# Holding four engines of the merge of a diffusion layer to the written order

## Chip, core and metric

The kernel runs on one core of one Trainium2 chip. The metric is device time in microseconds (us) from a launch of the whole layer, as the median of several runs. The profile is of one execution.

## What is computed

One layer over 2048 latent tokens of width 1024, with a context of 256 tokens. The part that the change touches is `branch_merge` and the residual behind it, and in the kernel the first operations of the channel sub-layer:

```python
def branch_merge(attn_o, gm_o, ga_logit, gb_logit, w_br_attn, w_br_gm, w_out):
    y = jax.nn.sigmoid(ga_logit) * (attn_o @ w_br_attn) + jax.nn.sigmoid(gb_logit) * (gm_o @ w_br_gm)
    return y @ w_out
...
    x = x + g1 * branch_merge(attn_x, gm_x, ga_x, gb_x, w_br_attn[l], w_br_gm[l], w_out[l])
    h2 = modulate(x, norm2_g[l], sh2, sc2)
    x = x + g2 * sq_relu_mlp(h2, w_ff1[l], w_ff2[l])
```

Here `attn_o` and `gm_o` are 2048 x 512, `w_br_attn` and `w_br_gm` 512 x 1024, `w_out` 1024 x 1024. Ahead of it lie the input projection, attention and the gated spatial mixing; behind it the MLP of width 4096.

## The kernel before

All matmuls take fp32 data as two rounded parts, a high part h and a remainder l = x - h, and make each product of three matmuls (`mm3`: h h, h l, l h). So each operand has a cast to h (ScalarE, L144, in some places VectorE) and a subtraction for l (L148, on GpSimd or VectorE): the function `split`.

The tokens are taken in four blocks (b = 0 to 3) of 512. In `merge` each block has two stages.

The first is the *branch product*. For each of eight steps m (128 output columns) TensorE makes two products in PSUM, of gated mixing ("g") and then of attention ("a"), each over four chunks k of the contraction: 24 matmuls of 128x512. VectorE multiplies both by their gates (L910, twice) and adds them (L913). ScalarE casts the sum to the high part of y, and GpSimd makes its remainder. Ahead of the matmuls of step m, `fetch` loads the raw weights and gates of two steps later and splits the weights: for each of "g" and "a" a cast on ScalarE and a remainder on GpSimd (on VectorE where block 0 calls it). Steps are counted through here, 0 to 31: block 1 has 8 to 15. Weights, raw and split, have the tag `bw` with 14 buffers (a step takes two raw and four split ones), gates have `gt` with 6.

The second is the *output product*, y times `w_out`. For each of four token tiles tt and two halves n of the columns, TensorE makes 24 matmuls over the eight parts of y. Of the first tile the parts 0 to 6 are taken for both halves ahead of part 7. After each half VectorE multiplies by the adaLN gate (L954) and adds to the residual tile `xt` (L955), and then `next(side, None)` issues one step of a side job. After each tile the sum goes to memory and ScalarE takes its sum of squares (L960).

In blocks 0 to 2 the side job is `br_inputs` of the next block: eight steps, one for each chunk of the branch inputs. Each loads a raw tile (and, for attention, a row of reciprocals, by which VectorE multiplies it in L848), casts it on ScalarE and makes the remainder on VectorE. The tag is `raw` (3 buffers) for what is loaded and `in` (16) for the parts.

In block 3 the side job is `h_early`, the head of the channel sub-layer for the first half of the tokens. Four of its steps begin with `turn(kk)`: VectorE scales a tile of 128 x 2048 (L992 in `h_scaled`), TensorE makes 16 transposes of it (L182), ScalarE takes the four results out of PSUM (L999). The other pieces (`combine`, `done`, `h_last`, `w1_plain`, `w1_combine`) are sums and splits on VectorE and ScalarE. The turns come after the first half of tile 0, the first half of tile 1, and both halves of tile 2:

```python
                    nc.vector.tensor_tensor(out=part, in0=ps, in1=self.g1b[:, cs], op=ALU.mult)
                    nc.vector.tensor_tensor(out=xt[:, cs], in0=xt[:, cs], in1=part, op=ALU.add)
                    next(side, None)
```

The program is a list of instructions in the written order. A planner then sets the order on each engine and on each DMA queue from modelled costs, with the written order as priority. `order` binds some of it by dependencies that cost no semaphore: buffers of one tag are first written in the written order, and an instruction that is "held" goes behind the one written before it on its engine. In the kernel before, held are a few short ranges (`pins`), TensorE and VectorE in attention (`fixed`), and SyncE in the second product of the MLP (`loads`). Nothing is held in `merge`. Transfers in `merge` are issued by SyncE, apart from the softmax sums, which ScalarE issues within block 0's branch product.

Of the kernel before, what the change touches and what calls it, by code (L numbers as in the profile page):

```python
# [67 lines left out]
class Kern:  # L68
    def __init__(self, ctx, tc, I, out):
        self.tc, self.nc, self.I, self.out = tc, tc.nc, I, out  # L70
        self.ctx = ctx
        self.uid = 0
        self.tags = {}
        self.pins = []
        self.fixed = []
        self.loads = []
        self.open_pools, self.pool_of = {}, {}
        self.banks = None
# [799 lines left out]
    def merge(self, first, start, last):  # L878
        nc = self.nc
        for _ in start:  # L880
            pass
        self.close("mid", "base")
        self.open("out")
        self.open("branch")
        steps = [(b, m) for b in range(NB) for m in range(KC)]
        it = iter(steps)
        q = []
        w_out = self.load_w_out()

        def fetch(lo_eng="pool"):  # L890
            s = next(it, None)
            if s is not None:
                q.append((self.br_weights(self.br_raw(s[1]), lo_eng), self.gate_in(*s)))

        inp = first
        early = [(s, self.br_raw(s[1])) for s in (next(it), next(it))]
        for s, raw in early:
            q.append((self.br_weights(raw, "dve"), self.gate_in(*s)))
        for b in range(NB):
            y = []  # L900
            for m in range(KC):
                fetch("pool" if b else "dve")
                ws, gt = q.pop(0)
                for nm in ("g", "a"):
                    ps = self.bank([TB])
                    wh, wl = ws[nm]
                    for k in range(4):
                        h, l = inp[nm][k]
                        self.mm3(ps, wh[:, k, :], wl[:, k, :], h, l, k == 0, k == 3)
                    nc.vector.scalar_tensor_tensor(  # L910
                        out=gt[nm], in0=gt[nm], scalar=1.0, in1=ps, op0=ALU.add, op1=ALU.mult
                    )
                nc.vector.tensor_tensor(out=gt["a"], in0=gt["a"], in1=gt["g"], op=ALU.add)  # L913
                yh, yl = self.sb("y", [TB], F32R), self.sb("y", [TB], F32R)
                self.split(gt["a"], yh, yl)
                y.append((yh, yl))
                if b == 0:
                    next(w_out, None)
                    if m == 2:
                        last.sums(self.sb("raw", [TB]))  # L920
                    if m == 4:
                        last.inverse()
            inp = {}
            if b + 1 < NB:
                side = self.br_inputs(b + 1, inp)
            else:
                self.close("branch", "pre")
                self.open("early", side="right")
                side = self.h_early()
                next(side)  # L930
            for tt in range(TT):
                tok = slice(tt * P, (tt + 1) * P)
                xt = self.sb("xt", [D])
                nc.sync.dma_start(xt, self.x_block(b)[tok, :])
                banks = [self.bank([512]) for _ in range(2)]

                def outer(n, ks):
                    cs = slice(n * 512, (n + 1) * 512)
                    for k in ks:
                        self.mm3(  # L940
                            banks[n], y[k][0][:, tok], y[k][1][:, tok], self.wo[k][0][:, cs],
                            self.wo[k][1][:, cs], k == 0, k == KC - 1,
                        )

                head = KC - 1 if tt == 0 else KC
                if tt == 0:
                    for n in range(2):
                        outer(n, range(head))
                for n in range(2):
                    cs = slice(n * 512, (n + 1) * 512)  # L950
                    ps = banks[n]
                    outer(n, range(head if tt == 0 else 0, KC))
                    part = self.sb("jk", [512])
# [3 lines that stand above are left out]
                nc.sync.dma_start(self.x1_d[b][tok, :], xt)  # L957
                junk = self.sb("jk", [D], mybir.dt.bfloat16)
                col = b * TT + tt
                nc.scalar.activation(  # L960
                    junk, xt, AF.Square, accum_out=self.ss2[:, col : col + 1]
                )
            for _ in side:
                pass

    def halves(self, kk, p, raw):
        nc = self.nc
        tag = "he" if (kk, p) in EARLY else "hl"
        h, l = self.sb(tag, [TB], F32R), self.sb(tag, [TB], F32R)
        nc.scalar.copy(h, raw)  # L970
        nc.vector.tensor_tensor(out=l, in0=raw, in1=f32(h), op=ALU.subtract)  # L971
        return h, l
# [469 lines left out]
    def order(self):  # L1442
        dep = mybir.DependencyInfo(mybir.DependencyClass.NoSync, mybir.DependencyReason.DATA)
        last, seen = {}, set()
        pinned = {n for r in self.pins for n in r}
        fixed = {n for r in self.fixed for n in r}
        loads = {n for r in self.loads for n in r}
        engines = (self.nc.tensor.engine, self.nc.vector.engine)
        for idx, i in enumerate(list(self.nc.cur_bb.bb.instructions)):
            keys = []  # L1450
            for o in i.outs:
                n = getattr(getattr(o, "bass_ap", None), "name", None)
                if n in self.tags and n not in seen:
                    seen.add(n)
                    keys.append(self.tags[n])
            held = idx in pinned or (idx in fixed and i.engine in engines)
            held = held or (idx in loads and i.engine == self.nc.sync.engine)
            after = keys + ([i.engine] if held else [])
            for prev in {last[k].name for k in after if k in last}:
                self.tc.add_manual_dep(i, prev, dep, reason="order")  # L1460
            for k in keys + [i.engine]:
                last[k] = i
# [242 lines left out]
```

## Time and profile before

| what | value |
|---|---|
| median of 3 runs | 3123.49 us (3121.77 to 3127.06) |
| the profiled execution | 3121.05 us |
| its span, first to last instruction | 3119.3 us |
| mean granted TensorE clock | 0.995 |
| TensorE busy | 3045.5 us (98%) |
| VectorE busy | 1937.7 us (62%) |
| ScalarE busy | 1352.0 us (43%) |
| GpSimd busy | 917.5 us (29%) |

The granted clock is the share of the full TensorE clock. PE is TensorE's matmul, PEld its weight load, DVE is VectorE, ACT ScalarE, POOL GpSimd, SP SyncE (SPq its queue of transfers). A line number such as L954 is that of the listing. In the profile `bw<-bw,bw` stands for the buffers that an instruction writes and reads, without their numbers. Matmul records overlap, so that TensorE's rate is better read from the distance of starts than from one duration. A bracket in a row of the timeline gives the engine's idle time ahead of the instruction and what ended it.

### The profile page before, as it was taken

What the parts mean: (1) busy time and instruction counts of PE and PEld (TensorE: products, weight loads), DVE (VectorE), ACT (ScalarE), POOL (GpSimd) and SP (SyncE); (2) the same over time, 40 slices, a digit from 0 to 9 for tenths busy, and PEclk for the clock granted to TensorE, in tenths of its full rate; (3) what the DMA queues carried; (4) which work ended last, traced back from release to release, by engine and by line L of the source; (5) the groups of instructions that cost most, each with busy time, mean ns of one, the idle gap of its engine ahead of it and who ended that gap; (6) DMA issues with size and microseconds to landing.
All of it is one profiled execution on the core that took longest, in us unless ns stands there. A gap on an engine that the chain in (4) does not pass through costs nothing.

```text
span 3119.3 us, 38046 instructions
## 1 busy us (share of the span) xinstructions
PE 3045.5 (98%) x13892; PEld 2299.1 (74%) x13892; DVE 1937.7 (62%) x2797; ACT 1352.0 (43%) x2058; POOL 917.5 (29%) x635
## 2 busy tenths in 40 slices
PE   7999999999999999999999999999999999999999
PEld 4888788877655555555777877887777788888777
DVE  4735666576677777677643478876654576654445
ACT  3353434433545454545322244444543344444433
POOL 1423324241688888888133300000000000000000
PEclk9999999999999999999999999999999999999999
DMA  6353555535100000002855448888576644445565
GB/s 202 112 177 119 200 166 172 188 93 188 38 14 5 18 11 18 11 5 91 272 161 161 151 145 314 313 306 280 190 259 204 216 149 154 158 147 194 206 215 203
DMA packets 332174, 485.42 MB, mean 156 GB/s; under 512 B 33969, under 2 KB 166321, under 8 KB 331986
## 3 DMA queue, kind: packets, MB, share of 16 engines
q1 hardware_dynamic: 324002, 478.38, 46.0%
q10 hardware_dynamic: 7984, 4.61, 0.5%
q8 instruction: 109, 1.79, 0.2%
q14 instruction: 79, 0.65, 0.1%
HBM read 348.56 MB, written 134.35 MB: 155 GB/s over the span
## 4 chain that ended last, share of the span: by engine, by line
PE 79%; DVE 7%; DMA 6%; POOL 3%; ACT 2%; issue 2%; SPq 0%; ACTq 0%; DVEq 0%; POOLq 0%
PE b L1196 12%; PE b L1197 12%; PE b L1195 11%; PE b L1597 8%; PE b L176 7%; PE b L178 7%; PE b L177 7%; PE b L1564 5%; PE b L1583 4%; PE b L1529 3%; PE b L182 2%; DMA bw<-in_w_br_gm 1%; DMA w<-in_w_in 1%; DVE f L1292 1%; DMA f<-ao_d 1%
## 5 line engine op out<-in xcount | busy, mean ns | idle before, releaser
L1292 DVE TENSOR_TENSOR f<-f,f 128x1024 fp32r<-128x1024 f32 x224 | 272.9, 1223 | 269.3 <-ACT f L1291 265.3
L1540 DVE TENSOR_REDUCE ts<-b 128x1 f32<-128x512 f32 x512 | 314.5, 681 | 172.6 <-PE b L1529 172.6
L1291 ACT CAST f<-f 128x1024 fp32r<-128x1024 f32 x224 | 235.2, 1053 | 330.8 <-DMA f<-ao_d 293.2
L1196 PE MATMUL b<-f,f 128*128 128x512 f32 x896 | 350.8, 392 | 5.1 <-DVE f L1292 4.6
L1197 PE MATMUL b<-f,f 128*128 128x512 f32 x896 | 348.9, 389 | 0.0
L1613 POOL TENSOR_TENSOR ac<-ac,p 128x512 f32<-128x512 f32 x216 | 296.3, 1403 | 70.7 <-ACT p L1587 69.5
L1195 PE MATMUL b<-f,f 128*128 128x512 f32 x896 | 306.6, 391 | 10.2 <-ACT b L1334 4.5
L1587 ACT ACTIVATE p<-b 128x512 f32<-128x512 f32 x384 | 199.6, 616 | 156.2 <-PE b L1583 153.4
L148 POOL TENSOR_TENSOR w<-w,w 128x1024 fp32r<-128x1024 f32 x60 | 148.6, 2477 | 399.5 <-ACT w L144 169.3
L1613 POOL TENSOR_TENSOR ac<-ac,t 128x512 f32<-128x512 f32 x160 | 232.5, 1478 | 0.1
L1196 PE MATMUL b<-hl,f 128*128 128x512 f32 x576 | 225.3, 391 | 2.2 <-DVE hl L971 2.1
L1195 PE MATMUL b<-hl,f 128*128 128x512 f32 x576 | 224.6, 390 | 0.0
L1197 PE MATMUL b<-hl,f 128*128 128x512 f32 x576 | 224.3, 390 | 0.0
L144 ACT CAST w<-w 128x1024 fp32r<-128x1024 f32 x120 | 125.9, 1049 | 217.4 <-DMA w<-in_w_in 181.3
L176 PE MATMUL b<-t,w 128*128 128x512 f32 x512 | 204.2, 399 | 5.7 <-DVE t L590 5.4
L1195 PEld LDWEIGHTS b<-f,f 128*128 128x128 f32 x896 | 167.5, 188 | 50.8 <-ACT f L1291 7.0
L1196 PEld LDWEIGHTS b<-f,f 128*128 128x128 f32 x896 | 168.2, 188 | 46.5 <-DVE f L1292 12.2
L178 PE MATMUL b<-t,w 128*128 128x512 f32 x512 | 200.9, 392 | 0.0
L177 PE MATMUL b<-t,w 128*128 128x512 f32 x512 | 200.5, 392 | 0.0
L1564 PE MATMUL b<-t,t 128*128 128x512 f32 x576 | 197.8, 413 | 0.8 <-ACT p L1587 0.5
L178 PE MATMUL b<-w,t 128*128 128x512 f32 (+1 forms) x528 | 192.0, 364 | 2.6 <-POOL t L148 2.5
L1197 PEld LDWEIGHTS b<-f,f 128*128 128x128 f32 x896 | 168.2, 188 | 34.4
(228 smaller groups left out, 6461.6 us busy)
## 6 DMA issues: line engine op xcount, KB each, us to landing
w<-in_w_in SPq DMA_DIRECT2D x120, 512.0 KB
ao_d<-f SPq DMA_DIRECT2D x224, 256.0 KB
f<-ao_d SPq DMA_DIRECT2D x112, 512.0 KB
f<-w2o_d SPq DMA_DIRECT2D x112, 512.0 KB
f<-in_w_ff SPq DMA_DIRECT2D x48, 1024.0 KB
w2o_d<-f SPq DMA_DIRECT2D x112, 256.0 KB
md<-in_w_mod SPq DMA_DIRECT2D x32, 512.0 KB
f<-x_d SPq DMA_DIRECT2D x64, 256.0 KB
```

What stands on the lines that cost most here:

```text
L176: mm(ps, sh, mh, start=start, stop=False)
L177: mm(ps, sh, ml, start=False, stop=False)
L178: mm(ps, sl, mh, start=False, stop=stop)
L1195: mm(ps, wh, hh, start=start and k == 0, stop=False, skip_group_check=True)
L1196: mm(ps, wh, hl, start=False, stop=False, skip_group_check=True)
L1197: mm(ps, wl, hh, start=False, stop=k == len(w) - 1, skip_group_check=True)
L1291: nc.scalar.copy(h, f32(l))
L1292: nc.vector.tensor_tensor(out=l, in0=f32(l), in1=f32(h), op=ALU.subtract)
L1540: nc.vector.tensor_reduce(out=self.mx[:, t, h, c : c + 1], in_=ps[h], axis=AX.X, op=ALU.max)
L1564: self.nc.tensor.matmul(self.pts[j][h], k.KA[c][self.kv][:, ks], self.qa[h], start=True, stop=False, skip_group_check=True,)
L1597: nc.tensor.matmul(self.o[h * HD : (h + 1) * HD, :], k.V[c][:, i, self.kv * HD : (self.kv + 1) * HD], pt[h], start=j == 0, stop=j == NKT - 1,)
L1613: nc.gpsimd.tensor_tensor(out=self.acc[e][:, h], in0=old[:, h], in1=pt[h], op=ALU.add)
```

## The change

A list `steady` gets one range: from the end of block 0's branch product to the end of `merge`. In `order` each instruction in that range is held behind the one written before it on its engine, except those on SyncE. No instruction is added, removed or changed.

```diff
@@ def __init__
         self.fixed = []
+        self.steady = []
         self.loads = []
@@ def merge
                     if m == 4:
                         last.inverse()
+            if b == 0:
+                begin = self.here()
             inp = {}
...
             for _ in side:
                 pass
+        self.steady.append(range(begin, self.here()))
@@ def order
         loads = {n for r in self.loads for n in r}
+        steady = {n for r in self.steady for n in r}
...
             held = idx in pinned or (idx in fixed and i.engine in engines)
+            held = held or (idx in steady and i.engine != self.nc.sync.engine)
             held = held or (idx in loads and i.engine == self.nc.sync.engine)
```

## The prediction

> **What bounds the kernel now.** I read the page first, for the engine that fills the span, then the busy time by stretch over the merge, then the waits of TensorE in it, and last the timelines around those waits.
>
> ```profile
> PE 3045.5 (98%) x13892; PEld 2299.1 (74%) x13892; DVE 1937.7 (62%) x2797; ACT 1352.0 (43%) x2058; POOL 917.5 (29%) x635
> ```
>
> TensorE is busy 98% of the span, so an edit counts only by the TensorE idle time, or slow TensorE time, that it takes away or adds. The stretches below are, in order, the output product of block 0, then branch products and output products of blocks 1 to 3, then the start of the channel sub-layer. Columns: stretch, its length, busy time of PE, PEld, DVE, ACT and POOL, granted clock, DMA share, GB/s.
>
> ```profile
> 1521.53:1565.05 43.52, 43.52 (x193) 36.05 (x192) 22.99 (x32) 11.66 (x21) 4.47 (x3) 1.00 0.70 234
> 1565.05:1608.57 43.52, 43.52 (x193) 36.05 (x192) 16.80 (x23) 11.33 (x20) 21.48 (x17) 1.00 0.49 151
> 1608.57:1659.87 51.30, 46.31 (x193) 36.88 (x192) 22.44 (x29) 11.64 (x20) 9.58 (x8) 0.97 0.56 180
> 1703.39:1755.03 51.64, 47.39 (x194) 37.61 (x193) 20.94 (x29) 11.62 (x20) 9.64 (x8) 0.93 0.49 163
> 1755.03:1798.55 43.52, 43.52 (x194) 36.05 (x193) 18.25 (x24) 10.90 (x19) 22.68 (x17) 1.00 0.52 161
> 1798.55:1849.13 50.58, 50.58 (x257) 42.85 (x256) 40.43 (x62) 21.28 (x34) 1.32 (x1) 1.00 0.37 122
> 1849.13:1880.70 31.57, 26.63 (x98) 18.27 (x97) 27.97 (x41) 19.27 (x32) 0.00 (x0) 0.95 0.61 211
> ```
>
> Each stretch of 192 matmuls takes 43.52 us undisturbed (0.227 us each; eight steps of 5.44 us). TensorE already runs the stages one behind the other in the written order. Two stretches are long: the output products of blocks 1 and 2 lose 51.30 - 43.52 = 7.78 and 51.64 - 43.52 = 8.12 us, together 15.9. Block 3's output product loses nothing: 50.58 is 192 matmuls plus 64 transposes.
>
> ```profile
> PE b L176 <- ACT y L144: 6.5, 2, 3.5
> PE b L178 <- POOL y L148: 2.6, 4, 1.0
> ```
>
> These two rows are all that TensorE waits for from 1522 to 1849 us: the casts and remainders of y, the last two of a block. The ScalarE timeline says why they are late:
>
> ```profile
> 1535.56 1.14 ACT L144 CAST bw<-bw 128x512 fp32r<-128x512 f32 x2
> 1607.68 0.62 ACT L144 CAST y<-gt 128x512 fp32r<-128x512 f32 x1
> 1612.04 0.62 ACT L144 CAST bw<-bw 128x512 fp32r<-128x512 f32 x1 [3.75 <-DMA bw<-in_w_br_gm]
> 1614.09 0.62 ACT L144 CAST bw<-bw 128x512 fp32r<-128x512 f32 x1 [1.43 <-POOL bw L148]
> 1614.61 1.13 ACT L144 CAST in<-raw 128x512 fp32r<-128x512 f32 x2
> 1615.65 0.61 ACT L144 CAST y<-gt 128x512 fp32r<-128x512 f32 x1
> 1618.92 0.62 ACT L144 CAST bw<-bw 128x512 fp32r<-128x512 f32 x1 [2.14 <-DMA bw<-in_w_br_gm]
> 1620.98 0.62 ACT L144 CAST bw<-bw 128x512 fp32r<-128x512 f32 x1 [1.44 <-POOL bw L148]
> 1624.16 0.62 ACT L144 CAST y<-gt 128x512 fp32r<-128x512 f32 x1 [2.04 <-DVE gt L913]
> ```
>
> The y casts of steps 14 and 15 (15 is the last of block 1) stand behind weight casts (bw) that wait for transfers, and behind input casts of the next block. The weight pairs run one step ahead of the text: from 1535.56 to 1618.92 there are nine pairs, steps 10 to 18, and the text has only steps 10 to 17 before y of step 15.
>
> **The change part by part.** No instruction is added or removed. On four engines, from block 0's output product to the end of the merge, each instruction goes behind the one written before it; SyncE's queue stays the planner's. So the parts are moves.
>
> *(a) The scaling at the head of each turn of `h_early`.* The lines, vector rows first:
>
> ```profile
> 1804.10 2.29 DVE L992 TENSOR_TENSOR f<-f,fs 128x2048 f32<-128x2048 f32 x1
> 1808.95 0.69 DVE L954 TENSOR_TENSOR jk<-b,g 128x512 f32<-128x512 f32 x1 [2.56 <-PE b L178]
> 1809.56 2.28 DVE L992 TENSOR_TENSOR f<-f,fs 128x2048 f32<-128x2048 f32 x1
> ...
> 1808.52 0.39 PE L178 MATMUL b<-wo,y 128*128 128x512 f32 x1
> 1808.75 1.91 PE L182 MATMUL b<-ident,f 128*128 128x128 f32 x16
> ```
>
> The text has, after the matmuls of a half n: L954, L955, L992, then 16 transposes, then the next half's matmuls. The planner keeps TensorE in that order but puts L992 (1804.10) ahead of L954 (1808.95), so the transposes start without a wait. Held in the written order, L954 must wait for the half's last matmul, L992 goes behind L955, and TensorE stands at the transposes, with the next matmuls queued behind them. Prices of the chain:
>
> ```profile
> 1849.33 0.69 DVE L954 TENSOR_TENSOR jk<-b,g 128x512 f32<-128x512 f32 x1 [4.02 <-PE b L178]
> 1850.06 0.69 DVE L955 TENSOR_TENSOR xt<-xt,jk 128x512 f32<-128x512 f32 x1
> ...
> 2175.60 2.30 DVE f L992
> 2177.91 0.04 issue
> 2177.95 1.97 PE b L182 x16
> ```
>
> L954 to L955 is 0.73 us; L955 to an independent instruction behind it 0.61 (as 1808.95 to 1809.56); L992 2.30; 0.05 to the first transpose. 0.73 + 0.61 + 2.30 + 0.05 = 3.7 us of idle TensorE, where there is none now. There are four turns: 4 x 3.7 = +14.8 us. Not less, since nothing else is ready on an engine in written order; more if VectorE is still busy with `combine` when the half ends, which by its four to seven instructions of 0.6 us in halves of 5.44 it is by 0.2 us at most.
>
> *(b) The slow clock behind such waits.* What a wait costs beyond its idle time:
>
> ```profile
> 1612.43 0.39 PE L178 MATMUL b<-wo,y 128*128 128x512 f32 x1
> 1616.32 0.50 PE L176 MATMUL b<-wo,y 128*128 128x512 f32 x1 [3.51 <-ACT y L144]
> ...
> 1618.76 0.63 PE L177 MATMUL b<-wo,y 128*128 128x512 f32 x1
> 1619.19 0.63 PE L178 MATMUL b<-wo,y 128*128 128x512 f32 x1
> ```
>
> Behind the 3.51 us wait matmuls start 0.43 us apart. In that stretch the lost 7.78 us are 51.30 - 46.31 = 4.99 idle and 2.79 slow; in block 2's they are 4.25 idle (longest wait under 3.5) and 3.87 slow. Bounds for each new wait: 0 and 3.9; I take 2.3, under the nearest row's 2.79 since a third of the slow time would fall on transposes. 4 x 2.3 = +9.2 us. The Trainium skill ("TensorE: Matmul & The Clock Gate", "What's actually happening") says that the clock is halved after an idle window of about 3.4 us in a free-running grid; a wait of 3.7 us then holds a whole window only about one time in ten, and the sum would be some 9 us lower. The stretch of block 2 speaks against so strict a reading: its clock is 0.93 with no wait over 3.5 us.
>
> *(c) The y casts of blocks 1 and 2.* In the written order y of step 15 stands behind pair 17, not 18, and no input cast comes between. But pair 10 is no longer made inside block 0's output product; it comes behind the last Square there. So at worst pairs 10 to 17 take the times that pairs 11 to 18 have now, and y goes at 1620.98 + 0.62 = 1621.60 instead of 1624.16: 2.5 us less on ScalarE, 1.9 of it left after GpSimd's queue (pair remainder first). The worst case supposes that pairs stay 6.6 us apart, as they are where the next raw pair needs the slots of the one being split:
>
> ```profile
> 1584.16 2.55 POOL L148 TENSOR_TENSOR bw<-bw,bw 128x512 fp32r<-128x512 f32 x2 [2.79 <-PE b L177]
> 1580.15 0.38 SPq L859 DMA_DIRECT2D bw<-in_w_br_gm  x1
> 1586.73 0.38 SPq L859 DMA_DIRECT2D bw<-in_w_br_gm  x1
> ```
>
> Two transfers 6.58 us apart, the second at the end of the split (1584.16 + 2.55 = 1586.71). bw has 14 slots and a step needs 6 (2 raw, 4 split). Three steps of split weights and one raw pair fill it, which is today's lead; with a step less, four slots come free as each step's products end, and raw pairs can load early, so the pairs can keep TensorE's 5.44. Then all 7.8 return. Between 1.9 and 7.8 a block I take 5, nearer to the full return because the slots allow it: 2 x 5 = -10 us (-3.8 to -15.9).
>
> *(d) Weights of block 3.* One step less of lead: six pairs from the last Square on (about 4 us into the stretch), 6.58 apart, and 2 to be split, make step 31 ready at 4 + 5 x 6.58 + 2 = 38.9 us, due at 7 x 5.44 = 38.1. +1 us (0 to 3).
>
> *(e) Inputs of the next block.* The last one (a, k = 3) now comes wholly behind the last L955 of an output product:
>
> ```profile
> 1549.99 0.69 DVE L848 TENSOR_TENSOR raw<-raw,raw 128x512 f32<-128x512 f32 x1 [1.64 <-DMA raw<-rs_d]
> 1551.43 0.69 DVE L148 TENSOR_TENSOR in<-raw,in 128x512 fp32r<-128x512 f32 x1 [0.74 <-ACT in L144]
> ```
>
> L954 and L955 1.4, then 1551.43 + 0.69 - 1549.99 = 2.1: ready 3.5 us after the product, needed 21 x 0.227 = 4.8 us after it. Hidden, with 1.3 us of cover; if the reciprocal's row lands late it costs up to 3 at each of three starts. +1 us.
>
> *(f) Start of the channel sub-layer.* 31.57 us for 98 matmuls (22.2) loses 9.3 already, by VectorE and ScalarE work that waits for the end of the merge in either order. Taken as 0 (-2 to +2).
>
> Sum: 14.8 + 9.2 - 10 + 1 + 1 = **+16 us**. The profiled execution took 3121.05 us (span 3119.3), 2.4 below the median of the runs, 3123.49. On the median that is 3139 us, 0.5% slower. Differences under 0.2% (6.2 us) I count as the same.
>
> **The rivals.**
>
> *The hold leaves the scaling where it is* (not slower). If L992 still gets ahead of L954, parts (a) and (b) vanish and (c) to (e) stay: -10 + 2 = -8, 3115 us, at best 3109. It decides at the order of the two instructions: L992 has to start 2.3 us before the half's last matmul ends. For it: the planner does so today. Against: the text binds each VectorE instruction to its forerunner, and SyncE alone is left out. 8%.
>
> *The waits cost their idle time alone.* The four waits come but the clock holds: 14.8 - 10 + 2 = +6.8, 3130; with the full return of (c) 14.8 - 15.9 + 2 = +0.9, 3124. For it: no wait in the table's undisturbed stretches. Against: both stretches with waits of 3 us or more show a clock under 1.00. 17%; the reading of the Trainium skill in (b) belongs here.
>
> *The weights become the bound.* Pairs stay 6.6 us apart or SyncE, planned for other times, holds raw pairs back behind stores: -3.8 instead of -10, and +3 each for (d) and three starts (e), slow clock at 3.9 a turn: 14.8 + 15.6 - 3.8 + 3 + 5 = +34.6, 3158. For it: 6.58 between transfers today. Against: the slots. 17%.
>
> **How the numbers follow.** The forecast, 58%, spans 3131 to 3147 ((c) from 4 to 7.5 a block and (b) from 1.3 to 3). From 3122 to 3156 I expect eight in ten: below lie the first rival and the last of the second, above the end of the third. Faster by over 0.2% (under 3117.2): the first rival, 0.08. Within it (to 3129.7): the half of the second with much returned and a little of the forecast's low end, 0.14. Slower: 0.78.
>
> **What would show it.** Block 3's output product grows from 50.6 to about 74 us, with four waits of TensorE on L992 of 3.5 to 4 us and a clock near 0.8 to 0.9 there. Output products of blocks 1 and 2 shrink to 44 to 49 us, with y casts directly behind two weight casts. Branch products of blocks 1 to 3 stay at 43.5, or grow by 1 to 4 with waits on bw. I am wrong if L992 shows no wait, if the clock stays at 1.00 there, or if the time moves after 1880 us.

## Result and the profile after

The changed kernel took 3136.99 us (median of 5 runs, 3135.33 to 3138.84) against 3123.25 us for the kernel before (five runs by now): a ratio of 1.0042, 95% interval 1.0027 to 1.0057. It is slower by 0.4%, as forecast (3139 us, 0.5%).

In the changed listing the lines stand one to four lower: L954, L955 and L992 are L957, L958 and L996, L144 and L148 are L145 and L149, L182 is L183, L859 and L874 are L860 and L875.

The busy time by stretch over the merge of the changed kernel: block 0's output product, then the output products of blocks 1, 2 and 3, then the start of the channel sub-layer. Columns as in the prediction.

```profile
1527.67:1571.19 43.52, 43.52 (x193) 36.04 (x192) 19.91 (x30) 9.61 (x17) 1.29 (x1) 1.00 0.62 205
...
1614.71:1658.23 43.52, 43.52 (x193) 36.04 (x192) 18.04 (x26) 7.91 (x14) 3.06 (x3) 1.00 0.48 157
...
1701.76:1745.28 43.52, 43.52 (x194) 36.04 (x193) 18.14 (x26) 7.91 (x14) 3.23 (x3) 1.00 0.47 157
...
1788.80:1862.02 73.22, 57.98 (x258) 48.21 (x257) 40.38 (x61) 21.68 (x34) 1.32 (x1) 0.91 0.27 87
1862.02:1893.08 31.06, 25.92 (x98) 18.33 (x97) 27.60 (x41) 18.52 (x31) 0.00 (x0) 0.95 0.55 194
```

The two long output products (51.30 and 51.64 us) are at 43.52, the whole 15.9 us returned. The branch products between them are at 43.5 us too. Block 3's output product has grown from 50.58 to 73.22 us, +22.6. Its TensorE idle time was nothing and is 73.22 - 57.98 = 15.24 us; the other 57.98 - 50.58 = 7.40 are a slow clock (0.91). The next stretch, 31.06 us for 31.57, is unchanged but for half a microsecond.

TensorE's waits from 1500 to 1920 us, the first rows:

```profile
PE b L183 <- DVE f L996: 11.5, 3, 4.1
PE b L183 <- issue: 3.8, 1, 3.8
```

These are four waits at the transposes, three put down to the scaling and one, as long, to no releaser; there too the transposes start (1847.70) just behind the end of the scaling (1845.32 + 2.28 = 1847.60). The waits for y are gone. The first of the four in the timelines, VectorE, then TensorE, and the transposes of the other three:

```profile
1799.19 0.69 DVE L957 TENSOR_TENSOR jk<-b,g 128x512 f32<-128x512 f32 x1 [4.89 <-PE b L179]
1799.92 0.69 DVE L958 TENSOR_TENSOR xt<-xt,jk 128x512 f32<-128x512 f32 x1
1800.53 2.29 DVE L996 TENSOR_TENSOR f<-f,fs 128x2048 f32<-128x2048 f32 x1
...
1798.77 0.39 PE L179 MATMUL b<-wo,y 128*128 128x512 f32 x1
1802.87 2.59 PE L183 MATMUL b<-ident,f 128*128 128x128 f32 x16 [3.71 <-DVE f L996]
1805.11 0.78 PE L177 MATMUL b<-wo,y 128*128 128x512 f32 x1
1805.69 0.63 PE L178 MATMUL b<-wo,y 128*128 128x512 f32 x1
1806.11 0.63 PE L179 MATMUL b<-wo,y 128*128 128x512 f32 x1
...
1816.35 2.45 PE L183 MATMUL b<-ident,f 128*128 128x128 f32 x16 [3.71 <-DVE f L996]
1834.90 3.54 PE L183 MATMUL b<-ident,f 128*128 128x128 f32 x16 [4.06 <-DVE f L996]
1847.70 2.98 PE L183 MATMUL b<-ident,f 128*128 128x128 f32 x16 [3.75 <-issue]
```

VectorE had been idle for 4.89 us when the half's last matmul let L957 go, and L996 stood two places behind it. The 16 transposes then take 2.59 us instead of 1.91, and the next matmuls start 0.58 and 0.42 us apart instead of 0.23. ScalarE at the end of block 1's branch product:

```profile
1613.18 1.14 ACT L145 CAST bw<-bw 128x512 fp32r<-128x512 f32 x2 [0.64 <-DMA bw<-in_w_br_gm]
1617.06 0.62 ACT L145 CAST y<-gt 128x512 fp32r<-128x512 f32 x1 [2.74 <-DVE gt L914]
1617.58 1.14 ACT L145 CAST in<-raw 128x512 fp32r<-128x512 f32 x2
```

The last y of the block waits for its gate product and nothing else: 1617.06 is 2.35 us after the branch product's end at 1614.71. Before, it was cast 15.6 us after it (1624.16 against 1608.57). From the last y of block 0 to this one ScalarE casts nine pairs of weights where it cast ten before: the step of lead is gone.

By these stages of the merge alone the profiles differ by 22.6 - 15.9 = +6.7 us. Their spans differ by 14.2. Most of the rest, 6.1 us, lies ahead of the held range, where the order of every engine and queue is the same: block 0's output product starts at 1527.67 instead of 1521.53.

### The profile page after: what moved, and what is told of

Read it like the earlier page. It is cut to its first block, busy times and chain, and to the rows that moved or that the text cites. A ratio compares the mean times of both kernels' runs of the same rounds, so it can differ in the third digit from the quotient of the medians.

```text
span 3133.5 us, 38040 instructions
## 1 busy us (share of the span) xinstructions
PE 3052.1 (97%) x13892; PEld 2308.6 (74%) x13892; DVE 1948.6 (62%) x2797; ACT 1352.6 (43%) x2058; POOL 915.3 (29%) x635
## 4 chain that ended last, share of the span: by engine, by line
PE 79%; DVE 9%; DMA 5%; issue 3%; ACT 2%; POOL 2%; SPq 0%; ACTq 0%; DVEq 0%; POOLq 0%
PE b L1200 11%; PE b L1201 11%; PE b L1199 11%; PE b L177 8%; PE b L1603 8%; PE b L179 8%; PE b L178 8%; PE b L1570 5%; PE b L1589 4%; PE b L1535 3%; PE b L183 2%; DMA w<-in_w_in 1%; DMA f<-w2o_d 1%; DVE f L1296 1%; POOL t L394 1%
## 5 line engine op out<-in xcount | busy, mean ns | idle before, releaser
L149 POOL TENSOR_TENSOR w<-w,w 128x1024 fp32r<-128x1024 f32 x60 | 147.2, 2453 | 402.4 <-ACT w L145 171.0
L145 ACT CAST w<-w 128x1024 fp32r<-128x1024 f32 x120 | 125.8, 1049 | 223.1 <-DMA w<-in_w_in 200.4
```

## The experiments

Theory: the return comes from ScalarE, which no longer runs a step ahead with weight casts or casts inputs in front of y; the cost is that the scaling stands behind L954 and L955 on VectorE, and that the clock falls in the waits. The rivals are named with each. Ratios are to the kernel before on the same chip.

**Holding up to block 3's output product, and holding only it.** The first ends the range ahead of the last output product, the second begins it there.

```diff
             if b == 0:
                 begin = self.here()
+            if b + 1 == NB:
+                self.steady.append(range(begin, self.here()))
...
-        self.steady.append(range(begin, self.here()))
```
```diff
-            if b == 0:
+            if b + 1 == NB:
                 begin = self.here()
```

> The hold ends ahead of block 3's output product; the rest of the change stays. If the cost lies in the four waits on the scaling alone, this kernel has the return and not the cost: 3123.3 - 15.9 = 3107 us, block 3's output product back at 50.6 us, no wait of TensorE on the scaling, the six stretches before it at 43.5 us each. If holding costs some 6 us ahead of the held range as well (the profile of the changed kernel is 6.1 us late there), it takes 3113 to 3114 us and block 0's output product starts near 1527.7 us again instead of 1521.5.

> The hold begins only at block 3's output product. If the two effects add, the cost comes without the return: 3123.3 + 22.6 = 3146 us, with block 3's output product at 73 us, four waits of 3.7 to 4.1 us on the scaling, and blocks 1 and 2 losing 7.8 and 8.1 us in their output products as before. If the return and the cost depend on each other (a later start of the last stage), between 3137 and 3143 us. With 6 us more ahead of the range, 3152 us.

The first took 3111.05 us, 0.9957 (0.9945 to 0.9970); the second 3152.98 us, 1.0087 (1.0073 to 1.0101). Stretches of the output products, blocks 2 and 3 of the first kernel, then blocks 1 to 3 of the second:

```profile
1702.57:1746.10 43.53, 43.53 (x193) 36.04 (x192) 17.83 (x26) 7.92 (x14) 2.95 (x3) 1.00 0.50 157
1789.62:1840.21 50.59, 50.59 (x258) 42.84 (x256) 40.42 (x62) 21.29 (x34) 1.32 (x1) 1.00 0.38 126
```
```profile
1619.95:1669.96 50.01, 46.29 (x193) 36.90 (x192) 22.22 (x29) 11.52 (x20) 8.59 (x7) 0.97 0.57 184
1713.48:1764.65 51.17, 47.19 (x193) 37.60 (x192) 21.60 (x29) 11.52 (x20) 9.28 (x8) 0.93 0.51 165
1808.17:1883.70 75.53, 60.29 (x257) 50.54 (x256) 40.37 (x60) 22.49 (x34) 1.32 (x1) 0.86 0.27 84
```

Cost and return separate cleanly and each is where it was said to be. The times are 4 and 7 us above the first expectations (3107 and 3146), which were worked out from 3123.3 us. From the kernel before on the same chip, 3125.74 us, the stages give 3125.74 - 15.9 = 3109.8 and, with block 3's output product at 75.53, 3125.74 + 24.95 = 3150.7; 1 and 2 us remain.

**VectorE free; ScalarE alone held; VectorE alone held.** Only the condition in `order` is changed:

```diff
-            held = held or (idx in steady and i.engine != self.nc.sync.engine)
+            held = held or (
+                idx in steady and i.engine not in (self.nc.sync.engine, self.nc.vector.engine)
+            )
```
```diff
+            held = held or (idx in steady and i.engine == self.nc.scalar.engine)
```
```diff
+            held = held or (idx in steady and i.engine == self.nc.vector.engine)
```

> TensorE, ScalarE and GpSimd are held over the whole range, VectorE is left to the planner. If the cost is that the scaling stands behind L954 and L955 on VectorE, the four waits go and block 3's output product takes 50.6 us. If the return comes from ScalarE's order (y ahead of the later weight casts), blocks 1 and 2 keep their 43.5 us: 3107 us in all. If part of the return was VectorE's (gate products no longer behind the remainders of the next block's inputs), 2 to 5 us of it go at each of the two blocks: 3111 to 3117 us. If the waits come from TensorE's or ScalarE's hold, 3137 us as in the changed kernel.

> Only ScalarE is held over the range. If the return comes from ScalarE no longer casting the weights of the third step ahead in front of y, the output products of blocks 1 and 2 take 43.5 to 44.5 us, block 3's 50.6 (the scaling is free to go ahead), and the kernel 3110 to 3115 us. If TensorE's or GpSimd's hold was needed for it, 2 to 6 us are lost again in each of the two: 3116 to 3126 us.

> Only VectorE is held over the range. By the place of the scaling alone block 3's output product takes 73 to 76 us with four waits of 3.7 to 4.1 us. Blocks 1 and 2: if ScalarE's lead is the whole cause of the late y, they lose 6 to 8 us each as before, and the kernel takes 3145 to 3153 us; if the remainders of the next block's inputs in front of the gate products on VectorE had a share, they lose 2 to 5 us each, 3138 to 3144 us.

VectorE free took 3115.23 us, 0.9968 (0.9956 to 0.9980), with output products of 43.52, 43.52 and 50.58 us: by its stages the return is whole, though the time alone lies in the range named for a share of VectorE's (3111 to 3117). ScalarE alone took 3112.56 us, 0.9959 (0.9946 to 0.9972); VectorE alone 3147.84 us, 1.0077 (1.0058 to 1.0097). Output products of blocks 1 to 3, ScalarE alone held, then VectorE alone:

```profile
1615.40:1658.92 43.52, 43.52 (x194) 36.04 (x192) 19.58 (x28) 8.21 (x15) 2.54 (x2) 1.00 0.53 175
1702.44:1745.96 43.52, 43.52 (x194) 36.04 (x193) 19.40 (x28) 8.21 (x15) 2.28 (x2) 1.00 0.46 156
1789.48:1840.06 50.58, 50.58 (x257) 42.85 (x256) 40.22 (x62) 21.08 (x34) 1.32 (x1) 1.00 0.42 137
```
```profile
1613.46:1662.24 48.78, 45.58 (x193) 36.95 (x192) 17.65 (x26) 10.90 (x19) 8.94 (x8) 0.97 0.54 173
1705.76:1754.48 48.72, 45.59 (x193) 36.88 (x192) 17.50 (x26) 10.91 (x19) 8.82 (x7) 0.96 0.54 173
1798.00:1873.50 75.50, 60.21 (x257) 50.36 (x256) 40.26 (x60) 21.85 (x34) 1.32 (x1) 0.86 0.25 81
```

One engine gives the whole return and another the whole cost. VectorE's order also has a part in the late y: held alone it leaves 5.2 us lost in each of blocks 1 and 2 instead of 7.8 and 8.1, since the gate products no longer stand behind the remainders of the next block's inputs. That is between the two expectations, and the time lies in the first. What stays is the y of step 14, still behind the weights of step 17 and an input cast (1619.44 against the branch product's end at 1613.46). With ScalarE held the part needs no hold of VectorE. How ScalarE's return divides between the weight casts and the input casts in front of y is not shown by any run.

**The scaling one turn ahead, all four engines held.**

```diff
         def turn(kk):
-            self.h_scaled(x[kk], rb)
...
+        self.h_scaled(x[0], rb)
         yield
         turn(0)
+        self.h_scaled(x[1], rb)
...
         turn(1)
+        self.h_scaled(x[2], rb)
...
         turn(2)
+        self.h_scaled(x[3], rb)
```

> As the changed kernel, all four engines held, but the text of h_early issues each scaling one turn earlier (the first ahead of the stage, the second and third right behind the transposes of the turn before, the fourth behind those of the third). If the place of the scaling on VectorE is the whole cost, the four waits go with the order held: block 3's output product 50.6 to 53 us, 3109 to 3113 us in all. If TensorE stands at the transposes for another reason (banks, ScalarE's evictions, the tiles' arrival), waits of 1 to 3 us stay and the time is 3115 to 3125 us.

It took 3112.85 us, 0.9953 (0.9940 to 0.9966). Block 3's output product, and the head of its VectorE timeline:

```profile
1783.25:1833.83 50.58, 50.58 (x257) 42.86 (x256) 40.12 (x60) 21.08 (x34) 1.32 (x1) 1.00 0.39 126
```
```profile
1788.88 2.29 DVE L996 TENSOR_TENSOR f<-f,fs 128x2048 f32<-128x2048 f32 x1
1793.65 0.69 DVE L957 TENSOR_TENSOR jk<-b,g 128x512 f32<-128x512 f32 x1 [2.47 <-PE b L179]
1794.38 0.69 DVE L958 TENSOR_TENSOR xt<-xt,jk 128x512 f32<-128x512 f32 x1
1794.98 2.29 DVE L996 TENSOR_TENSOR f<-f,fs 128x2048 f32<-128x2048 f32 x1
```

The first scaling runs in VectorE's idle time ahead of L957, and the second behind L958 is that of the next turn. So the hold itself costs nothing; the written place of four instructions did.

**TensorE kept busy in the waits.** Behind each scaling, ahead of the transposes, 13 matmuls into a PSUM tile of their own are added.

```diff
             self.h_scaled(x[kk], rb)
+            ps = self.bank([512])
+            for _ in range(13):
+                nc.tensor.matmul(
+                    ps, self.wo[0][0][:, :P], self.wo[0][0][:, :512], start=True, stop=True
+                )
```

> As the changed kernel, with 13 more matmuls on TensorE (13 x 0.227 = 2.95 us) in each of the four waits, whose result nobody reads; they end before the scaling does. If the slow clock is the answer to TensorE's idle time, the clock stays at 1.00 in block 3's output product, which takes 50.6 + 15.2 = 66 us instead of 73 to 75.5, and the kernel 7 to 10 us less than the changed one: 3126 to 3129 us. If the slow time comes with the transposes or with the work behind them whatever TensorE does in the wait, 3134 to 3137 us; if the matmuls get in the way of the scaling, up to 3148 us.

It took 3126.76 us, 1.0003 (0.9993 to 1.0014), 9 us less than the changed kernel's 3135.97 in its second timing. The stretch of block 3's output product, and the first wait on TensorE:

```profile
1788.22:1855.06 66.84, 63.33 (x310) 52.32 (x308) 40.32 (x60) 21.19 (x34) 1.32 (x1) 1.00 0.30 95
```
```profile
1798.42 3.11 PE L1054 MATMUL b<-wo 128*128 128x512 f32 x13
1802.29 1.97 PE L183 MATMUL b<-ident,f 128*128 128x128 f32 x16 [0.77 <-DVE f L996]
```

With the same chain on VectorE the clock stays at 1.00, the transposes take 1.97 us, and the stretch is 66.84 us, 6.4 to 8.7 less than without the idle work. So the slow time is the clock's answer to idle TensorE.

**More and fewer buffers for the branch weights.** `"bw": 16` in the kernel before, `"bw": 12` in the changed one, instead of 14.

> The kernel before, nothing held in the merge, with 16 buffers for the branch weights instead of 14. If the late y of blocks 1 and 2 come from raw weights that wait for the buffers of the pair being split, two more buffers bring the pairs to TensorE's pace: the two output products lose 0 to 3 us each instead of 7.8 and 8.1, and the kernel takes 3110 to 3116 us. If they come from the order on ScalarE alone (y behind the pair of the third step ahead and behind input casts), the losses stay at 5 to 8 us each and the time at 3122 to 3127 us.

> The changed kernel, all four engines held, with 12 buffers for the branch weights instead of 14. If the written order returns the two waits because two buffers are free for the next raw pair while a pair is split, these 12 put the raw pair behind the split again: the branch or output products of blocks 1 to 3 lose 4 to 12 us in each block, 3148 to 3170 us in all. If the order alone does it, they lose 0 to 2 us each: 3136 to 3142 us.

The kernel before with 16 took 3134.55 us, 1.0023 (1.0012 to 1.0034); the changed one with 12 took 3137.14 us, 1.0038 (1.0024 to 1.0051). Output products of blocks 1 and 2 with 16 buffers and no hold, and ScalarE's casts around the last y of block 1 there; then, with 12 and the hold, block 1's output product and ScalarE's last casts of block 1:

```profile
1619.06:1672.29 53.23, 47.72 (x193) 37.20 (x192) 23.04 (x29) 13.21 (x23) 11.32 (x9) 0.94 0.54 178
1715.81:1768.85 53.04, 47.67 (x193) 37.65 (x192) 22.41 (x29) 13.32 (x23) 11.25 (x9) 0.94 0.50 164
...
1631.39 1.14 ACT L144 CAST bw<-bw 128x512 fp32r<-128x512 f32 x2 [3.54 <-DMA bw<-in_w_br_gm]
1633.45 0.62 ACT L144 CAST in<-raw 128x512 fp32r<-128x512 f32 x1 [0.93 <-DMA raw<-gm_d]
1636.58 0.62 ACT L144 CAST y<-gt 128x512 fp32r<-128x512 f32 x1 [2.50 <-DVE gt L913]
```
```profile
1616.20:1659.72 43.52, 43.52 (x193) 36.05 (x192) 17.43 (x26) 8.95 (x16) 6.73 (x5) 1.00 0.54 177
...
1620.84 1.14 ACT L145 CAST bw<-bw 128x512 fp32r<-128x512 f32 x2 [4.97 <-DMA bw<-in_w_br_gm]
1621.88 0.61 ACT L145 CAST y<-gt 128x512 fp32r<-128x512 f32 x1
```

Two more buffers do not bring the return. The losses are 9.7 and 9.5 us, and the time lies above both expectations. In four profiles with the order of the kernel before in blocks 1 and 2 (its two, the one held only in block 3's output product and the one with memsets below) the losses are 6.5 to 7.8 and 7.7 to 9.7 us, so only block 1's is clearly longer. The lead is the same: between the last y of blocks 0 and 1 ScalarE casts ten pairs with 14 buffers and ten with 16, and an input cast last. The pairs' transfers are further apart, 8.1 us on average (1587.25 to 1627.60, five steps) instead of 7.2 (1580.15 to 1616.08); why the planner set them so is not shown. So this run does not tell what free buffers would do if transfers came at TensorE's pace.

The run with 12 does tell. In the changed kernel the transfers come every 5.5 us (1581.90 to 1614.85, six steps), about TensorE's 5.44. With 12 buffers they are 6.6 us apart on average (1584.70 to 1617.48, five steps), and nothing is lost: the last y goes 5.7 us behind the branch product (1621.88 against 1616.20), in time for part 7 of the first tile, which is due 42 matmuls, 9.5 us, into the output product. My idea that free buffers make the return falls. The order on ScalarE makes it: the last y came late where the weights of step 18 and input casts stood in front of it, with 14 and with 16 buffers, and in time where the weights of step 17 were the last, with 14 and with 12.

**Both kernels once more, and the kernel before with six memsets on GpSimd.**

```diff
-        self.nc.gpsimd.memset(self.sb("pd", [120]), 0.0)
+        pd = self.sb("pd", [120]); self.nc.gpsimd.memset(pd, 0.0)
...
-        self.ffn()
+        self.ffn(); [self.nc.gpsimd.memset(pd, 0.0) for _ in range(6)]
```

> The changed kernel once more. If the 6.1 us ahead of the held range are a matter of the execution, block 0's output product starts anywhere from 1521 to 1528 us, and the rest (from there to the end) takes 1605 to 1607 us. If they belong to the program, it starts at 1527 to 1528.5 us again. Time 3135 to 3139 us, or 3130 to 3133 us if the profiled chip run was late by chance.

> The kernel before once more, for its profile. If the first 1521 us differ only from execution to execution, block 0's output product starts between 1522 and 1530 us this time (the five held kernels: 1525 to 1533), and the stages from there to the end take what they took before, 1597 to 1600 us. If the held kernels are late by themselves, it starts at 1521 to 1523 us again.

> The kernel before with six more small memsets on GpSimd that nothing waits for; the order of the other engines and of the transfers is the same. If the kernels other than the one before are some 4 us slower than their stages say because a different program as such runs its first 1520 us more slowly, this one takes 3128 to 3131 us. If not, 3124 to 3127 us as before.

The changed kernel took 3135.97 us, 1.0032 (1.0020 to 1.0043); the kernel before 3124.79 us, 0.9994 (0.9984 to 1.0004); the one with memsets 3126.89 us, 1.0003 (0.9992 to 1.0014). From the start to block 0's output product and from there on, the kernel before and then the changed one:

```profile
0.00:1529.10 1529.10, 1491.12 (x7045) 1029.60 (x7045) 979.26 (x1614) 691.01 (x1171) 825.29 (x566) 0.99 0.32 101
1529.10:3128.37 1599.27, 1561.65 (x6849) 1275.69 (x6847) 965.03 (x1184) 660.52 (x888) 91.76 (x69) 0.99 0.60 207
```
```profile
0.00:1525.04 1525.04, 1487.30 (x7044) 1025.47 (x7045) 971.07 (x1613) 690.98 (x1170) 826.47 (x566) 0.99 0.32 101
1525.04:3129.16 1604.12, 1560.33 (x6849) 1278.95 (x6847) 967.78 (x1184) 662.66 (x889) 89.18 (x69) 0.99 0.61 207
```

The same program needs 1521.5 us for its first part in one execution and 1529.1 in another; the changed one 1527.7 and 1525.0. In the kernel with the memsets, with the same order on the other engines, it is 1535.5. So the 6.1 us ahead of the range in the first pair of profiles lie within what executions differ by, and are not shown to be an effect of the change. From block 0's output product to the end it is 1597.73 and 1599.27 against 1605.86 and 1604.12: +8.1 and +4.9, on average +6.5 us. The timings give +13 (8 to 18) and +10 us (6 to 13). The 3.5 to 6.6 us between the profiles' difference and the medians' stay open. Worked out in the same way, from the kernel before on the same chip and the stages of the profile, the medians of all kernels with a hold lie 1 to 7 us above their stages. The kernel with memsets, at +0.9 us (-2.5 to +4.4), speaks against the idea that any other program is some 4 us slower.

## Why the prediction was right, and where it was not

The direction and both mechanisms held. The time held too, but in part by luck, as the sum at the end shows. By its steps:

(a) was right: 3.7 us of idle time a turn were worked out from the four rows, 3.71, 3.71, 4.06 and 3.75 are there, 15.24 us for 14.8. The one longer wait is VectorE still at work from the piece before, 0.35 us where 0.2 were allowed. The experiments with one engine held and with the scaling ahead show it.

(b) was right in kind, and the size depends on the execution: 7.40 us in one profile and, by 75.55 - 50.58 - 15.24, 9.7 in the other, for 9.2. These are the second profile's row and its idle time, 75.55 - 60.31:

```profile
1786.15:1861.70 75.55, 60.31 (x258) 50.50 (x256) 40.34 (x60) 22.44 (x34) 1.32 (x1) 0.86 0.26 84
```

The reading of the Trainium skill that was weighed there ("TensorE: Matmul & The Clock Gate", "What's actually happening": half the clock after an idle window of about 3.4 us) would have had such waits nearly free. Half the clock is what the matmuls show (0.42 us apart instead of 0.23). But all five profiles with the four waits show a clock of 0.86 to 0.91, and the kernel with 16 buffers shows 0.94 with no wait above 1.8 us, so the measurement decides against that strict reading, and with it against the second rival.

(c) was the mis-sized term: -15.9 for -10, the far end of its bounds. The worst case took the old times of the weight pairs and moved them by one step. Under the hold the two casts of a pair stand together and the pairs come earlier: the weights of step 17 are cast 1.5 us before block 1's branch product ends (1613.18 against 1614.71), where they were cast 5.5 us after it (1614.09 against 1608.57). The prediction's reason for leaning towards a full return is half right. The transfers did come at TensorE's pace, but the return does not need it: with 12 buffers y is in time too. The lead on ScalarE was named in the prediction; that holding ScalarE is enough alone was not seen.

(d) and (e) were priced at 1 us each and are nothing: all branch products are at 43.5 us. (f) was right (31.06 for 31.57).

With the terms as measured the sum is 15.2 + 7.4 - 15.9 = +6.7, with the second profile's clock +9, not +16. The medians moved by 13.7 and 10.2. So the forecast of 3139 for 3137 was nearer than its parts, and that is luck: (c), (d) and (e) were too pessimistic by 8 us, and part of that is covered by the 3.5 to 6.6 us that the stages do not explain. By the terms as measured the time would be 3130 to 3133 us, around the low end of the forecast's range.

Two of the prediction's sums do not come out as written. The third rival puts 3 us on each of three starts in (e), which is 9 and not 5, so that it ends at 3162. The forecast's upper end, with (c) at 4 a block and (b) at 3 a turn, is 3144 and not 3147. Neither bears on the result. Its table of stretches leaves out block 2's branch product (1659.87 to 1703.39), which is at 43.52 too.

## What to carry to other kernels

Before an engine is held to the written order, read for each instruction what it would stand behind: an operation that is ready early (the scaling) and that another engine's queue waits for must be written ahead of the one that waits for that other engine. A planner's lead is no gain where the leading operation waits for a transfer on the engine that also makes the next operand of the bound engine; a deeper pool (16 buffers) did not shorten the loss. Holding one engine (ScalarE here, 0.9959), ending the range ahead of the last stage (0.9957) or moving four instructions (0.9953) turned a change of +0.4% into -0.4%; these three are not told apart by their intervals.

## What the runs showed of the hardware

TensorE's clock fell at every wait at the transposes. In the five profiles with the four waits these are 20, of 3.0 to 4.8 us, and the 16 transposes behind them took 2.45 to 3.68 us instead of 1.91. Shorter waits do not follow one length: behind one of 2.07 us (in the kernel held only in block 3's output product, 1525.74) matmuls started 0.43 us apart, and behind one of 2.52 us (in the kernel with memsets, 1529.58) 0.24 us from the fourth on. 13 matmuls without use, leaving 0.8 to 1.2 us of wait, kept the clock up, and saved 6.4 to 8.7 us over four waits. And the first half of an unchanged program, with the same order on each engine, took from 1521.5 to 1529.1 us in two profiled executions, more than the +6.5 us of the change from there on.
